# A transformer layer on one core: context's squares summed on VectorE, and three steps of attention and pooling asked for at other times

## The chip, the core and the metric

The kernel runs on one core of a Trainium2 chip. The metric is the device time in microseconds of one execution; lower is better. The core's engines work side by side: TensorE (PE in the profile, its weight loads PEld), VectorE (DVE), ScalarE (ACT), GpSimd (POOL), and SyncE (SP), which issues the transfers from HBM into the on-chip memory (SBUF). Matmuls write into PSUM, which has eight banks here.

## What is computed

One layer over 256 latent tokens and 256 context tokens, width 2048, all in float32. Cut to what matters:

```python
mod   = silu(c)     @ w_mod + b_mod          # sa, ca, ga, sm, cm, gm of the latent tokens
mod_c = silu(c_ctx) @ w_mod + b_mod
h_c = rmsnorm(ctx) * norm_attn_w * (1 + ca_c) + sa_c
h   = rmsnorm(x)   * norm_attn_w * (1 + ca)   + sa
# q, k, v, pooled input, gates: columns of h @ w_in; context gives keys and values only
q, k = rope(rmsnorm(q)), rope(rmsnorm(k));  k_c = rmsnorm(k_c)
heads = softmax(q1 k1^T) - lam * softmax(q2 k2^T), times v       # 8 heads, 512 keys
y_a = rmsnorm(heads) @ w_a_up
y_b = pool(p) @ w_b_up        # 4 groups: (mean over a window of 2, 4, 8, 16) - p, then a 256x256 product
x = x + ga * ((sigmoid(g_a) * y_a + sigmoid(g_b) * y_b) @ w_o)
x = x + gm * (relu(modulate(x) @ w_ff1) ** 2 @ w_ff2)
```

The norm `rmsnorm` divides by the root of the mean of squares over the 2048 channels of a token.

## The kernel before, in words

**Arithmetic.** A float32 weight chunk (128x1024, 512 KB) comes into a `raw` buffer (five of them), ScalarE casts it to a high part `whi` (line 224) and VectorE subtracts to get a low part `wlo` (line 225); a product is three matmuls of high and low parts. The raw buffer is free when the subtraction is done. For the modulation weights `w_m` the raw chunk itself is the matmul's operand.

**Order of the work.** The whole program is traced first, and then a planner of the framework gives every engine its own queue: of the instructions whose inputs its model of time takes as ready, the one earliest in the program goes first. So an instruction can get ahead of others that stand before it in the program. Three things hold that in check: instructions in `pin(...)` keep the program's order among themselves; with `ordered_pe` on, TensorE keeps the program's order altogether (it is on for the modulation stage and off after it); and a tile of a ring must wait until an earlier tile of that ring is given up. The ring `work` (tag `w2`) has nine buffers of 128x512 floats and serves nearly everything small: squares, raw keys, exponentials, pooled sums and differences. On the engine a queue is then worked off strictly in order.

**Transfers** are in one list (`plan`), which `load_next` walks; `wchunk` hands out the next chunk and loads two (at first three) chunks ahead. Each `wchunk` call is also one tick: `later(n, fn)` puts `fn` into the program n ticks on.

**Modulation stage** (loop over f = 0 to 15). `mod_tile(f)` takes four raw chunks and multiplies them with both conditioning vectors, and ScalarE copies the `rows` out (line 366). `mod_columns` turns rows into columns, and `hidden(f, t, ...)` makes slice f of the normed hidden tokens (lines 388 to 390), which needs `rms[t]`, the reciprocal root of the mean squares. `rms[0]` (latent) is made before the loop. Context arrives as four transfers `cT`, planned among the weights of f = 2 and 3. At f = 4 its squares are taken in four calls of `square_sums` (lines 459 to 469): two squares of 128x512 on ScalarE, their sum on VectorE, and two products with the constant matrix `mean` for each, so eight products of 128x256 add up in PSUM (`ssq`). Then come `rsq`, and context's slices 0 to 6 along with f = 4 to 6. Between the parts of an f, TensorE works off `steps`: products for keys and queries of group 0 (heads 0 to 3), as far as hidden slices are ready.

**Keys and queries.** `qk_evac` copies a product of 128 tokens out of PSUM, takes squares, norms and rotates, and `later(wait, turn)` asks for the four transposes (`qkT`, line 453) that bring it to `kT` or `qT`. After the modulation stage this is done for four key tiles (wait 2 + t) and two query tiles (6 + t). Meanwhile `v_group(0)` runs: eight chunks of `w_v`, 24 matmuls each (16 with the high part of the weights, eight with the low part).

**Main stretch.** `run(bulk, side, EVERY)` walks through the chunks of `q_group(1)`, `k_group(1)`, `v_group(1)`, `pooling()` and `gates()`. Every chunk yields a weight (0 for q, 4 for k and v, 2 in pooling and gates); whenever the sum has grown by EVERY = 4.4, one step of `attention` goes into the program: the scores of a head and 128 queries (`sc`, four matmuls), maxima on VectorE, exponentials on ScalarE, and the transposes (`aTp`) and value product (`ob`) of earlier steps. Steps of heads 4 to 7 must wait until all six tiles of group 1 are turned; such a step does nothing. At the same time `late_gen` streams the other modulation weights through VectorE (`macc`, line 581, pinned).

**Pooling.** For group g, four chunks of `w_p` give `pin` in PSUM. ScalarE copies it to `za`, GpSimd adds shifted copies (line 745) to window sums, and `later(3, ...)` asks for `pool_diff`: edge corrections on VectorE (line 757, pinned, at the start; line 759, not pinned, at the end), the difference `d` (line 761), and its split into `dh` (ScalarE, line 248) and `dl` (VectorE, line 249). `pool_out(g)` multiplies these with `pool_w`; groups 2 and 3 have it within the first chunks of `gates`.

After this come the output projection, the norm, and the MLP (`ff1`, `ff2`), which the diff does not touch.

Of the kernel before, what the change touches and what calls it, by code (L numbers as in the profile page):

```python
# [12 lines left out]
F32R = mybir.dt.float32r  # L13
# [7 lines left out]
T = 256  # L21
# [27 lines left out]
def layer(ctx: ExitStack, tc, a, out):  # L49
# [21 lines left out]
    def bank(name):  # L71
        return psum.tile([P, 512], F32, tag="ps", name=name)

    def work(name, shape=None, dt=F32):
        return pool.tile(shape or [P, 512], dt, tag="w2", name=name, bufs=9)
# [19 lines left out]
    def later(n, fn):  # L95

        waiting.append([n, fn])
# [284 lines left out]
    def hidden(f, t, c3):  # L382

        src, h = ((xT, hL), (cT, hC))[t]
        u = work("hw", [P, T])
        ht, k8 = h[f // 8], f % 8
        bias = c3[:, 1, t:t + 1]
        vec.scalar_tensor_tensor(u, src[:, f, :], c3[:, 0, t:t + 1], rms[t], ALU.mult, ALU.mult)
        act.activation(ht[:, 0, k8, :], u, AF.Identity, bias=bias)
        vec.scalar_tensor_tensor(ht[:, 1, k8, :], u, bias, ht[:, 0, k8, :].bitcast(F32), ALU.add, ALU.subtract)  # L390

    def tokens(nt):
        return [(hL, 0), (hL, 1), (hC, 0), (hC, 1)][:nt]
# [5 lines left out]
    def xstat(w, banks, toks, nk=8, last=1):  # L399

        for ch in range(nk - last + 1):
            n = last if ch == nk - last else 1
            chunks = [wchunk(*w, ch + i, ahead=AHEAD - i) for i in range(n)]
            order = [(i, kk, t) for i in range(n) for kk in range(2) for t in range(len(banks))]
            if ch == nk - last:
                order.sort(key=lambda o: o[2])
            groups = [order] if n == 1 else [[o for o in order if o[2] == t] for t in range(len(banks))]  # L410
            for group in groups:
                for part in range(2):
                    for i, kk, t in group:
                        k = 2 * (ch + i) + kk
                        h, tt = toks[t]
                        wt = chunks[i][part][:, kk * 512:kk * 512 + 512]
                        if part == 0:
                            pe.matmul(banks[t], tok(h, k, 0, tt), wt, start=k == 0, stop=False)  # L418
                            pe.matmul(banks[t], tok(h, k, 1, tt), wt, start=False, stop=False)  # L419
                        else:  # L420
                            pe.matmul(banks[t], tok(h, k, 0, tt), wt, start=False, stop=k == 2 * nk - 1)  # L421
            yield len(banks)
# [4 lines left out]
    def qk_evac(ps, tt, g, dest, tab, wait):  # L427
        raw = work("qraw")
        act.copy(raw, ps)
        sq = work("qsq")  # L430
        act.activation(sq, ps, AF.Square)
        ss = small("qss", 8)
        vec.reduce_sum(ss, sq.rearrange("p (h d) -> p h d", d=64), axis=AX.X)
        r = rsq(ss, 8, 1.0 / 64)
        r3 = raw.rearrange("p (h d) -> p h d", d=64)
        vec.tensor_mul(r3, r3, r.unsqueeze(2).broadcast_to([P, 8, 64]))
        if tt < 2:
            sq3 = sq.rearrange("p (h d) -> p h d", d=64)
            for ax in range(2):
                for b in range(2):  # L440
                    o = ax * 32 + b * 16
                    i = ax * 32 + (1 - b) * 16
                    vec.tensor_mul(sq3[:, :, o:o + 16], r3[:, :, i:i + 16],
                                   tabs[:, tab + 1, tt, o:o + 16].unsqueeze(1).broadcast_to([P, 8, 16]))
            vec.tensor_mul(r3, r3, tabs[:, tab, tt, :].unsqueeze(1).broadcast_to([P, 8, 64]))
            gp.tensor_add(raw, raw, sq)
        else:
            vec.tensor_mul(r3, r3, wkt.unsqueeze(1).broadcast_to([P, 8, 64]))

        def turn():  # L450
            pt = bank("qkT")
            for i in range(4):
                pin(pe.transpose(pt[:, i * P:i * P + P], raw[:, i * P:i * P + P], ident))
            act.copy(dest[:, 4 * g:4 * g + 4, tt * P:tt * P + P], pt.rearrange("p (i t) -> p i t", t=P))
            turned[g] += 1

        later(wait, turn)

    def square_sums(src, eng, sb, i):

        sq = [work("sq") for _ in range(2)]
        for h in range(2):
            k = 4 * i + 2 * h
            xs = src[:, k:k + 2, :].rearrange("p a t -> p (a t)")
            act.activation(sq[h], xs, AF.Square)
        eng.tensor_add(sq[0], sq[0], sq[1])
        return lambda: [pin(pe.matmul(sb[:, 0:T], mean, sq[0][:, h * T:h * T + T], start=(i + h == 0), stop=(i + h == 4)))
                        for h in range(2)]
# [25 lines left out]
    PACE = (0, 0, 4, 4, 6, 6, 8, 8) + (6,) * 8  # L494

    cols = {}

    context = {4: (0, 1), 5: (2, 3, 4), 6: (5, 6)}
    ordered_pe[0] = True
# [4 lines left out]
    for f in range(KT):  # L504
        if f % 2 == 0:
            ps = bank("mod")
        rows = mod_tile(f, ps)
        if f == 4:
            sb = bank("ssq")
            for i in range(4):  # L510
                square_sums(cT, vec, sb, i)()
            rms.append(rsq(sb[:, 0:T], T, P / D, "rms"))
        j = 2 if f == 6 else -1 if f == 5 or f % 2 == 0 else f // 2
        if j >= 0:
            for w in ("w_k", "w_q"):
                held[w, j] = wchunk(w, 0, j, ahead=FIRST_AHEAD if j < 7 else 1)
        steps(PACE[f] // 2)
        cols[f] = mod_columns(f, rows)
        steps(PACE[f] - PACE[f] // 2)
        hidden(f, 0, cols[f])  # L520
        for k in context.get(f, (f,) if f > 6 else ()):
            hidden(k, 1, cols[k])
        if f == 10:
            tables()
    lasts = [pair_steps(n, 7) for n in ("kx", "q", "kc")]
# [6 lines left out]
    qT = s8("qT", [P, NH, T])  # L532
    kT = s16("kT", [P, NH, 2 * T])
    for t in range(4):
        qk_evac(kb[t], t, 0, kT, 2, 2 + t)
    for t in range(2):
        qk_evac(qb[t], t, 0, qT, 0, 6 + t)

# [73 lines left out]

    def v_group(g):
        bs = [bank(f"v{g}_{t}") for t in range(4)]
        yield from xstat(("w_v", g), bs, tokens(4))
        for t in range(4):
            act.copy(v[:, t, g * 512:g * 512 + 512], bs[t])
        values[0] += 4
# [99 lines left out]
    def pooling():  # L718
        yb = pairtile("yb")
        ybh[0] = yb  # L720
        diff.clear()
        for g, w in enumerate(WINDOWS):
            ps = bank("pin")
            for i in range(2):
                for kc in range(2):
                    hi, lo = wchunk("w_p", 2 * g + i, kc)
                    for kk in range(8):
                        k = 8 * kc + kk
                        sl = slice(kk * P, kk * P + P)
                        mm3(ps[:, i * T:i * T + T], hi[:, sl], lo[:, sl], act_slice(hL, k, 0), act_slice(hL, k, 1),  # L730
                            k == 0, k == KT - 1)
                    if g > 1 and i == 0 and kc == 1:
                        pool_out(g - 2)
                    yield 2
            s0 = 8 - w // 2
            sums = []
            for i in range(2):
                src, oth = work("za", [P, T + 16]), work("zb", [P, T + 16])
                gp.memset(src[:, 0:8], 0.0)
                gp.memset(src[:, T + 8:T + 16], 0.0)  # L740
                act.copy(src[:, 8:T + 8], ps[:, i * T:i * T + T])
                step, n = 1, T + 16
                while step < w:
                    n -= step
                    gp.tensor_add(oth[:, 0:n], src[:, 0:n], src[:, step:step + n])
                    src, oth = oth, src
                    step *= 2
                sums.append(src[:, s0:s0 + T])
            later(3, partial(pool_diff, g, w, ps, sums))

    def pool_diff(g, w, ps, sums):

        d = work("d")
        n0, n1 = w // 2, w // 2 - 1
        e0 = PRM["edge"][0] + sum(x - 1 for x in WINDOWS[:g]) * 2
        for i, s in enumerate(sums):
            pin(vec.tensor_mul(s[:, 0:n0], s[:, 0:n0], prm[:, e0:e0 + n0]))
            if n1:
                vec.tensor_mul(s[:, T - n1:T], s[:, T - n1:T], prm[:, e0 + n0:e0 + n0 + n1])
            sl = slice(i * T, i * T + T)  # L760
            vec.scalar_tensor_tensor(d[:, sl], s, 1.0 / w, ps[:, sl], ALU.mult, ALU.subtract)
        dh = work("dh", dt=F32R)
        dl = work("dl", dt=F32R)
        split(dh, dl, d)
        diff.append((dh, dl))

    def pool_out(g):
        dh, dl = diff[g]
# [322 lines left out]
```

## Time and profile before

| | us |
|---|---|
| median of 3 runs | 1505.93 (1504.83 to 1506.88) |
| the profiled execution | 1506.33 |
| its span, first to last instruction | 1504.5 |
| TensorE busy | 1457.1 |
| VectorE busy | 992.0 |
| ScalarE busy | 694.6 |
| GpSimd busy | 120.7 |
| mean granted clock of TensorE | 0.991 |

Times in the views are microseconds from the span's start, and a timeline line reads: start, duration, engine, source line, operation, output <- inputs, shape, count; in brackets the idle time of the engine just before, and what ended it. Several like instructions in a row are one line with a count (x8); its duration then runs from the first start to the last end. L67 is the wrapper through which instructions with a written-out order go. Modulation lasts until about 143 us, the values of group 0 until 197, pooling and gates of group 0 until about 460, and from there on TensorE hardly waits.

### The profile page before, as it was taken

The page shows a single profiled execution, that of the slowest core. Times are in us where ns is not written, and L with a number is a line of the kernel's source. Part 1 is how long each engine was busy: PE and PEld are TensorE (multiplying, and loading weights), DVE is VectorE, ACT ScalarE, POOL GpSimd, SP SyncE. Part 2 cuts the span into 40 slices and gives each one's busy share as a digit, 9 for nine tenths or more (in the row PEclk, how much of TensorE's full clock was granted, in tenths as well). Part 3 has the DMA queues.
Part 4 walks back from the last instruction along what each step waited for, and adds up shares of the span by engine and source line. Part 5 has one row for each costly group of instructions (what it writes and reads, how often), then busy time and mean ns, then how long its engine had stood idle before and what let it go on. Part 6 is the DMA issues. An engine that isn't in the chain of part 4 may idle for free.

```text
span 1504.5 us, 20036 instructions
## 1 busy us (share of the span) xinstructions
PE 1457.1 (97%) x7592; PEld 1205.5 (80%) x7592; DVE 992.0 (66%) x1216; ACT 694.6 (46%) x956; POOL 120.7 (8%) x120
## 2 busy tenths in 40 slices
PE   5899999999899999999989999999999999999998
PEld 3567787678878888888879988888888888888887
DVE  3465968877877776666766765666666555555575
ACT  3334344646654444444534545535445453544532
POOL 0000101100320000000000100100000010000260
PEclk8999999999999999999999999999999999999999
DMA  9798687366578778788756677677776666656564
GB/s 377 296 345 324 195 284 247 98 210 208 169 234 295 255 262 273 249 304 282 213 159 203 226 247 239 210 248 229 246 236 215 192 189 194 188 192 193 186 194 141
DMA packets 97440, 347.85 MB, mean 231 GB/s; under 512 B 11072, under 2 KB 11712, under 8 KB 97344
## 3 DMA queue, kind: packets, MB, share of 16 engines
q1 hardware_dynamic: 96768, 345.50, 69.6%
q8 instruction: 59, 0.97, 0.3%
q0 software_dynamic: 576, 1.08, 0.2%
q14 instruction: 37, 0.30, 0.1%
HBM read 344.44 MB, written 2.10 MB: 230 GB/s over the span
## 4 chain that ended last, share of the span: by engine, by line
PE 87%; DVE 4%; DMA 4%; ACT 2%; issue 1%; POOL 1%; SPq 0%; DVEq 0%; ACTq 0%; POOLq 0%
PE f L940 14%; PE f L419 8%; PE f L418 8%; PE f L421 8%; PE f L943 7%; PE pg L419 3%; PE pg L418 3%; PE pg L421 3%; DMA raw<-in_w_m_dram 2%; PE w_k L67 2%; PE wo L419 2%; PE wo L421 2%; PE wo L418 2%; PE pyy L418 2%; PE pyy L419 2%; PE pyy L421 2%
## 5 line engine op out<-in xcount | busy, mean ns | idle before, releaser
L225 DVE TENSOR_TENSOR wlo<-raw,whi 128x1024 fp32r<-128x1024 f32 x443 | 547.9, 1239 | 360.4 <-ACT whi L224 337.6
L224 ACT CAST whi<-raw 128x1024 fp32r<-128x1024 f32 x443 | 463.9, 1048 | 574.2 <-PE f L419 184.9
L940 PE MATMUL f<-h,whi 128*128 128x512 f32 x896 | 224.2, 392 | 0.0
L418 PE MATMUL f<-whi,act 128*128 128x512 f32 x512 | 199.4, 389 | 0.0
L419 PE MATMUL f<-whi,act 128*128 128x512 f32 x512 | 199.3, 389 | 0.0
L940 PEld LDWEIGHTS f<-h,whi 128*128 128x128 f32 x896 | 161.7, 189 | 29.3
L581 DVE SCALAR_TENSOR_TENSOR macc<-raw,sil,macc 128x1024 f32<-128x1024 f32 x128 | 167.5, 1308 | 2.2 <-DMA macc<-in_b_ga_dram 1.9
L421 PE MATMUL f<-wlo,act 128*128 128x512 f32 x512 | 136.8, 389 | 0.0
L943 PEld LDWEIGHTS f<-h,wlo 128*128 128x128 f32 x896 | 122.3, 190 | 8.7
L943 PE MATMUL f<-h,wlo 128*128 128x256 f32 x896 | 124.9, 282 | 0.0
L421 PEld LDWEIGHTS f<-wlo,act 128*128 128x128 f32 x512 | 96.1, 188 | 19.9
L418 PEld LDWEIGHTS f<-whi,act 128*128 128x128 f32 x512 | 96.2, 188 | 19.9
L419 PEld LDWEIGHTS f<-whi,act 128*128 128x128 f32 x512 | 96.2, 188 | 19.7
L418 PE MATMUL pg<-whi,hL 128*128 128x512 f32 x256 | 100.6, 393 | 0.0
L419 PE MATMUL pg<-whi,hL 128*128 128x512 f32 x256 | 99.7, 390 | 0.0
L951 POOL TENSOR_TENSOR rsq<-relu 128x512 f32<-128x512 f32 x28 | 29.1, 1041 | 537.2 <-ACT relu L950 516.9
L421 PE MATMUL pg<-wlo,hL 128*128 128x512 f32 x256 | 68.6, 390 | 1.9 <-DVE wlo L225 1.9
L421 PEld LDWEIGHTS pg<-wlo,hL 128*128 128x128 f32 x256 | 48.0, 188 | 12.3 <-DVE wlo L225 2.4
L418 PEld LDWEIGHTS pg<-whi,hL 128*128 128x128 f32 x256 | 48.1, 188 | 10.1 <-issue 0.2
L419 PEld LDWEIGHTS pg<-whi,hL 128*128 128x128 f32 x256 | 48.1, 188 | 10.1 <-issue 0.2
L418 PE MATMUL wo<-whi,mix 128*128 128x512 f32 x128 | 49.9, 390 | 0.0
L419 PE MATMUL wo<-whi,mix 128*128 128x512 f32 x128 | 49.8, 389 | 0.0
(251 smaller groups left out, 2111.3 us busy)
## 6 DMA issues: line engine op xcount, KB each, us to landing
raw<-in_w_ff_dram SPq DMA_DIRECT2D x240, 512.0 KB, 4.3
raw<-in_w_m_dram SPq DMA_DIRECT2D x64, 512.0 KB, 8.0
raw<-in_w_ga_dram SPq DMA_DIRECT2D x32, 512.0 KB, 4.6
raw<-in_w_cm_dram SPq DMA_DIRECT2D x32, 512.0 KB, 4.4
raw<-in_w_gb_in_dram SPq DMA_DIRECT2D x32, 512.0 KB, 4.5
raw<-in_w_ga_in_dram SPq DMA_DIRECT2D x32, 512.0 KB, 4.7
raw<-in_w_sm_dram SPq DMA_DIRECT2D x32, 512.0 KB, 4.8
raw<-in_w_o_dram SPq DMA_DIRECT2D x32, 512.0 KB, 4.3
```

The costliest lines, as they stand in the source:

```text
L67: return (lambda *a, **k: pin(emit(*a, **k))) if self.flag[0] else emit
L224: act.copy(hi, raw)
L225: vec.tensor_sub(lo, raw, hi.bitcast(F32))
L418: pe.matmul(banks[t], tok(h, k, 0, tt), wt, start=k == 0, stop=False)
L419: pe.matmul(banks[t], tok(h, k, 1, tt), wt, start=False, stop=False)
L421: pe.matmul(banks[t], tok(h, k, 0, tt), wt, start=False, stop=k == 2 * nk - 1)
L581: pin(vec.scalar_tensor_tensor(acc, raw, sil[:, 0, k:k + 1], acc, ALU.mult, ALU.add))
L940: pe.matmul(ps, hi[:, kk * P:kk * P + P], both(h2, k), start=k == 0, stop=False)
L943: pe.matmul(ps[:, T:2 * T], lo[:, kk * P:kk * P + P], act_slice(h2, k, 0), start=False, stop=k == KT - 1)
L951: gp.tensor_mul(sq, r, r)
```

## The change

Four edits. Context's squares are taken by a new function `context_squares(i)`, called for quarters 0 and 1 after f = 2 and for quarters 2 and 3 after f = 3; VectorE keeps a running sum in one 128x512 tile, folds it to 128x256 at f = 4, and one product with `mean` follows. The key tiles of group 0 are turned a tick later. In `v_group(1)` the first two chunks yield the weights 0 and 2 instead of 4 and 4. The difference of pooling group 3 is asked for six ticks on instead of three, and the split of every group's difference is asked for one tick after the difference.

```diff
     cols = {}
+    total = []
+
+    def context_squares(i):
+
+        sq = [work("sq") for _ in range(2)]
+        for h in range(2):
+            act.activation(sq[h], cT[:, 4 * i + 2 * h:4 * i + 2 * h + 2, :].rearrange("p a t -> p (a t)"), AF.Square)
+        vec.tensor_add(sq[0], sq[0], sq[1])
+        if total:
+            vec.tensor_add(total[0], total[0], sq[0])
+        else:
+            total.append(sq[0])
...
         if f == 4:
+            sq = total[0]
+            vec.tensor_add(sq[:, 0:T], sq[:, 0:T], sq[:, T:2 * T])
             sb = bank("ssq")
-            for i in range(4):
-                square_sums(cT, vec, sb, i)()
+            pe.matmul(sb[:, 0:T], mean, sq[:, 0:T], start=True, stop=True)
             rms.append(rsq(sb[:, 0:T], T, P / D, "rms"))
...
             hidden(k, 1, cols[k])
+        if f in (2, 3):
+            for i in range(2):
+                context_squares(2 * f - 4 + i)
...
     for t in range(4):
-        qk_evac(kb[t], t, 0, kT, 2, 2 + t)
+        qk_evac(kb[t], t, 0, kT, 2, 3 + t)
...
         bs = [bank(f"v{g}_{t}") for t in range(4)]
-        yield from xstat(("w_v", g), bs, tokens(4))
+        for ch, w in enumerate(xstat(("w_v", g), bs, tokens(4))):
+
+            yield w if g == 0 or ch > 1 else 2 * ch
...
-            later(3, partial(pool_diff, g, w, ps, sums))
+            later(3 if g < 3 else 6, partial(pool_diff, g, w, ps, sums))
...
-        dh = work("dh", dt=F32R)
-        dl = work("dl", dt=F32R)
-        split(dh, dl, d)
-        diff.append((dh, dl))
+        diff.append((work("dh", dt=F32R), work("dl", dt=F32R)))
+        later(1, partial(split, *diff[-1], d))
```

## The prediction

> **What bounds the kernel now.** I read the page first, then the waits of TensorE, then the timeline at each place that the diff touches.
>
> ```profile
> span 1504.5 us, 20036 instructions
> PE 1457.1 (97%) x7592; PEld 1205.5 (80%) x7592; DVE 992.0 (66%) x1216; ACT 694.6 (46%) x956; POOL 120.7 (8%) x120
> PEclk8999999999999999999999999999999999999999
> PE 87%; DVE 4%; DMA 4%; ACT 2%; issue 1%; POOL 1%; SPq 0%; DVEq 0%; ACTq 0%; POOLq 0%
> ```
>
> TensorE is busy 1457.1 of 1504.5 us and makes 87% of the chain that ends last. Work taken off another engine gains nothing by itself; a change gains what it takes out of TensorE's queue or out of TensorE's waits. The waits of TensorE, in total us, times, and longest:
>
> ```profile
> PE mod L67 <- DMA raw<-in_w_m_dram: 13.5, 16, 3.0
> PE ssq L67 <- DVE sq L466: 9.6, 2, 7.2
> PE pin L254 <- DVE wlo L225: 4.3, 2, 2.9
> PE qkT L453 <- POOL qraw L446: 2.8, 3, 1.3
> PE sc L647 <- ACT e L652: 2.0, 1, 2.0
> PE pg L421 <- DVE wlo L225: 1.9, 1, 1.9
> PE sc L647 <- ACT qsq L431: 0.9, 1, 0.9
> ```
>
> Each part of the diff stands beside one of these rows: the squares beside ssq, the later turns of the keys beside qkT, the attention weights beside the two sc rows, the pooled differences beside pin and pg.
>
> **Part 1, context's squares.** This is the stretch of TensorE's queue in which the order is written out (the fourth slice of modulation weights, then the mean of squares, then the steps of keys and queries):
>
> ```profile
> 42.14 0.51 ACT L389 ACTIVATE hL<-hw,col 128x256 fp32r<-128x256 f32 x1 [1.14 <-DVE hw L388]
> 42.55 1.03 ACT L224 CAST first<-raw 128x1024 fp32r<-128x1024 f32 x1
> ...
> 43.61 1.23 DVE L225 TENSOR_TENSOR first<-raw,first 128x1024 fp32r<-128x1024 f32 x1 [0.45 <-ACT first L224]
> ...
> 44.87 4.67 SPq L212 DMA_DIRECT2D raw<-in_w_m_dram  x9
> ...
> 48.50 0.64 PE L67 MATMUL mod<-raw,cv 128*32 128x256 f32 x8 [2.01 <-DMA raw<-in_w_m_dram]
> 49.21 0.37 ACT L366 COPY rows<-mod 128x256 f32<-128x256 f32 x1 [4.68 <-PE mod L67]
> 49.47 3.75 ACT L465 ACTIVATE sq<-cT 128x512 f32<-128x512 f32 x7
> ...
> 51.49 6.35 PE L67 MATMUL ssq<-sq,mean 128*128 128x256 f32 x16 [2.35 <-DVE sq L466]
> ...
> 57.50 2.42 PE L67 MATMUL w_k<-first,hL 128*128 128x512 f32 x9
> ...
> 62.34 1.94 PE L67 MATMUL mod<-raw,cv 128*32 128x256 f32 x32
> ```
>
> TensorE ends f = 4 at 48.50 + 0.64 = 49.1, waits 2.35 us for squares that ScalarE begins only behind the copy of that f's rows, and then spends 6.35 us on 16 passes (two to each of eight products, 6.35 / 16 = 0.40 each). The diff leaves one product, two passes, 0.80 us, and puts the squares behind f = 2 and f = 3. Are they there in time? (An issue, the DMA view's line of context with its median us to landing, two lines of ScalarE's timeline, and the adds in the tile view with min/median/max ns.)
>
> ```profile
> 29.25 0.33 SPq L206 DMA_DIRECT2D cT<-in_cT_dram  x1
> ...
> cT<-in_cT_dram SPq DMA_DIRECT2D x4, 512.0 KB, 9.4
> ...
> 35.54 0.51 ACT L389 ACTIVATE hL<-hw,col 128x256 fp32r<-128x256 f32 x1 [1.14 <-DVE hw L388]
> ...
> 38.94 0.37 ACT L366 COPY rows<-mod 128x256 f32<-128x256 f32 x1 [2.90 <-PE mod L67]
> ...
> L466 DVE TENSOR_TENSOR sq<-sq x8: 691/692/693, 6.5 to 54.2; 128x512 f32<-128x512 f32 x8
> ```
>
> Context's last quarter is asked for at 29.25 and takes 9.4, so all of it lies there at 38.7. The first four squares fit on ScalarE between 36.05 (end of f = 2's last instruction) and 38.94: four by 3.75 / 7 = 0.54 is 2.14. The other four come behind 42.65; the last transfer that TensorE awaits lands at 48.50. VectorE's seven adds and one of half the width are 7 x 0.69 + about 0.4 = 5.2 us, against four adds, 2.8, now; it has 36 to 49 for them with little else. Their cover is that wait on DMA; were it gone, the last four squares and their adds would show, some 3 us.
>
> The cost is that the squares of f = 3 and the cast of the first key weights (42.55) want ScalarE in the same moment. That cast and its subtraction (43.61 to 44.84) free the raw buffer into which the transfer of 44.87 goes, and this is the one that lands at 48.50. Each square that gets ahead of it moves everything by 0.54; the cast stands earlier in the program, so I count one: TensorE begins ssq at 49.6 and ends at 50.4.
>
> Then the clock. Windows in rows: length, busy PE, PEld, DVE, ACT, POOL, granted clock, DMA share, GB/s.
>
> ```profile
> 46.70:50.10 3.40, 0.64 (x8) 0.16 (x8) 0.00 (x0) 0.89 (x3) 0.00 (x0) 0.99 0.99 377
> 50.10:53.50 3.40, 2.01 (x5) 1.67 (x6) 2.08 (x3) 3.12 (x7) 0.00 (x0) 0.50 1.03 417
> 53.50:57.00 3.50, 3.50 (x10) 2.75 (x9) 0.69 (x1) 0.63 (x1) 0.00 (x0) 0.52 1.02 406
> ...
> 64.00:70.00 6.00, 6.00 (x50) 4.43 (x46) 2.76 (x8) 2.32 (x6) 0.00 (x0) 1.00 0.49 175
> ...
> 398.30:401.70 3.40, 3.40 (x16) 3.40 (x17) 3.36 (x4) 3.40 (x10) 0.35 (x1) 0.51 0.74 230
> ```
>
> From 50.1 to 57.0 the clock is 0.5, and the ssq passes run in it. Without them the key steps stand in that low time. From 57.50 to 62.34 they and their company take 4.84 us at full clock. If the clock comes back at 53.5, then 50.4 to 53.5 does 1.55 of it, 3.29 is left, and f = 5 starts at 56.8 instead of 62.34: 5.5 us. If it comes back at 57.0, as before, 3.3 is done by then, f = 5 starts at 58.5: 3.8. If it never drops, 55.2: 7.1. I take 5.5, since after the stall near 398 one full window sufficed, and here the first window is now full too. The Trainium skill, "TensorE: Matmul & The Clock Gate", Part 1 on the clock gate, speaks against part of the gain: what is issued in the first 3.4 us or so after idling runs at half rate, and one busy window restores it. By that rule the sum has 5.5, by the rows at 50 to 57 it would have 3.8; the row of 398.30 agrees with the rule.
>
> Is it kept? The transfers for f = 5 to 7 were queued from 44.87 on, and 64 to 70 shows the DMA half idle (0.49), waiting for buffers that TensorE frees. From there on each wait for w_m follows TensorE's own releases, so all of it moves together. Counted: 5.5, bounds 3.0 (four squares ahead of the cast: ssq at 51.25 to 52.05, two low windows, f = 5 at 59.3) and 7.1.
>
> **Part 2, keys of group 0 turned a chunk later.**
>
> ```profile
> 157.15 0.66 PE L453 MATMUL qkT<-prm,qraw 128*128 128x128 f32 x4 [1.31 <-POOL qraw L446]
> 162.13 0.65 PE L453 MATMUL qkT<-prm,qraw 128*128 128x128 f32 x4 [0.89 <-POOL qraw L446]
> ```
>
> The two transposes stand 4.98 us apart, about one chunk of w_v; a chunk later covers 1.31 and 0.89. The last key now falls due with the first query, and attention starts only in k_group(1), so nobody waits for them. A qraw buffer is held 5 us longer. Gain 2.2; bounds a loss of 1.3 (one more wait of that size, for a buffer) and 2.2.
>
> **Part 3, attention pauses.** In v_group(1) the weights 4, 4 of the first two chunks become 0, 2; EVERY is 4.4. Summed, the seventh and eighth steps move from chunks 1 and 2 to chunks 3 and 4. The ninth and tenth steps were empty before (they waited for group 1's turns); now only the ninth is, so head 4 begins after chunk 6 as before, and every later step comes 0 or 1 chunk later. What it moves away from:
>
> ```profile
> 282.19 1.12 PE L647 MATMUL sc<-kT,qT 64*128 64x512 f32 x2 [0.88 <-ACT qsq L431]
> ...
> 286.86 1.12 PE L647 MATMUL sc<-kT,qT 64*128 64x512 f32 x2 [1.97 <-ACT e L652]
> 289.67 0.67 DVE L448 TENSOR_TENSOR qraw<-qraw,wkt 128x512 f32<-128x512 f32 x1
> ```
>
> The first scores wait for a PSUM bank that the last key's square still reads, the second for VectorE's maxima, which queue among the keys' norms; these end at 290.3. Three chunks in, both are past. Gain 0.88 + 1.97 = 2.85; bounds a loss of 2.0 (one more wait of that size, with the turns of chunks 3 to 6) and 2.85.
>
> **Part 4, pooling.** Group 3's difference is asked for six chunks on instead of three, each group's cast one chunk after its difference.
>
> ```profile
> 425.82 0.58 DVE L759 TENSOR_TENSOR za<-za,prm 128x7 f32<-128x7 f32 x1 [2.53 <-POOL za L745]
> 429.27 0.17 DVE L759 TENSOR_TENSOR za<-za,prm 128x7 f32<-128x7 f32 x1 [2.87 <-POOL za L745]
> 429.38 1.23 DVE L225 TENSOR_TENSOR wlo<-raw,whi 128x1024 fp32r<-128x1024 f32 x1
> 430.66 1.20 PE L421 MATMUL pg<-wlo,hL 128*128 128x512 f32 x4 [1.94 <-DVE wlo L225]
> ```
>
> VectorE stands 2.53 + 2.87 us at edge products whose sums GpSimd has not done; the gate weights' low part is queued behind them, and TensorE waits 1.94. L759 is not pinned and takes no new buffer, so the planner may put it there again: I take half, 1.0. The other side: sums, differences and casts hold their buffers of the nine-deep work ring longer, while heads come up to a chunk later. A new stall there would be priced like the longest in the pin row, 2.9, with a window at half clock behind it (398.30: 3.4 us, 1.7 lost): 4.6. Bounds: gain 2, loss 4.6.
>
> **The sum.** 5.5 + 2.2 + 2.85 + 1.0 = 11.55. The profiled execution took 1506.33 (span 1504.5 and 1.83 around it), 0.40 above the median of the runs, 1505.93. So 1494.8 for the like of that execution, 1494.4 for the median.
>
> **Rivals.**
> *The squares do not move.* ScalarE took no square before the rows of f = 4, though all of context was there at 38.7; if what held them (the work ring hands out buffers in program order) is not it, they run at 49.47 again, seven adds behind them, and the one product ends near 57.4 instead of 57.84. Part 1 gives 0.4, the time 1499.5. Against it: they now stand ahead of f = 4's rows in the program.
> *The casts go behind the squares.* The bound of 3.0 in part 1: 1496.9. It decides as soon as the planner thinks the key weights land after hL of f = 3.
> *Slower.* Part 4's longer-held buffers: every group's copy out of PSUM and every difference needs work buffers that the previous group's cast gives back. With a cast a chunk later at each of four groups, a weight's low part is stuck behind a difference each time: 4 x 4.6 = 18.4, less 10.55 of the other parts, 1513.8. It decides from three such stalls on (13.8 against 10.55 + 3). For it: pin and pg show that this already happens three times. Against: they are three in the whole kernel, 6.2 us, and heads come at most one chunk later.
>
> **How the numbers follow.** Forecast 0.60, squares unmoved 0.12, casts behind squares 0.13, slower 0.08, and 0.07 for pooling losses that about cancel the gain. The range: below, part 1 at 7.1, pooling at 2 and some more shifting, 1490; above, part 1 at 0.4, part 3 at nothing, 1502. A difference of 0.2%, 3 us, is about what a measurement here tells from none. Faster by more: 0.83; within: 0.09; slower: 0.08.
>
> **What would show it.** ssq for context as two passes right behind f = 4, without a wait on sq; w_k behind it partly at 0.5; f = 5 near 57. No qkT wait near 157 and 162. The scores of the seventh step near 285 on the new clock without waits. In pooling, L759 of width 7 without idle time ahead of it, pg waits gone. I am wrong if ssq still begins behind the rows' copy by 5 us or more, if the transfer that f = 4 awaits lands 2 us later than 48.5, or if new waits of TensorE between 380 and 460 add up to more than the 1.9 of pg.

## The result, and the profile after

The changed kernel takes 1490.85 us (median of 4 runs, 1490.53 to 1492.22) against 1506.41 of the kernel before beside it (1504.83 to 1509.66): a ratio of 0.9896, interval 0.9878 to 0.9913. That is 15.6 us where 11.5 were forecast; the time lies in the range, near its lower end. The profiled execution took 1492.22, 14.1 less than the one before. One execution below, the profiled one of the changed kernel with a transfer on GpSimd's queue, took 4145.31 us where its other five took 1491.66 to 1494.04; its ratio leaves it out, and its trace isn't used. The page of the changed kernel:

```profile
span 1490.4 us, 19996 instructions
...
PE 1450.0 (97%) x7578; PEld 1201.2 (81%) x7578; DVE 992.8 (67%) x1220; ACT 694.3 (47%) x956; POOL 121.2 (8%) x120
...
PE 90%; DMA 4%; DVE 3%; ACT 1%; issue 1%; SPq 1%; POOL 0%; DVEq 0%; POOLq 0%; ACTq 0%
```

VectorE and ScalarE do what they did, as squares and sums only moved. TensorE lost 14 passes of ssq and some slow ones. Its waits (us in total, times, longest):

```profile
PE mod L67 <- DMA raw<-in_w_m_dram: 15.6, 20, 2.3
PE ssq L67 <- DVE sq L466: 7.0, 1, 7.0
PE pin L254 <- DVE wlo L225: 5.6, 2, 3.3
...
PE late L617 <- ACT e L671: 1.5, 1, 1.5
```

The second wait for squares is gone (the one left is that of the latent tokens at the start), and so are qkT, both sc rows and pg (the gates' products). But w_m rose from 13.5 to 15.6 and pin from 4.3 to 5.6, and a wait of `late` (products that sum up the late modulation weights) of 1.5 stands where there was one of 0.5. Where the time went shows better by stretches between landmarks of TensorE's timeline, whose ends lie on the same instruction in both traces (us, each rounded by itself; forecast beside them):

| stretch | before | after | less | forecast |
|---|---|---|---|---|
| start to the end of f = 4 | 49.1 | 47.9 | 1.3 | 0 |
| end of f = 4 to first values | 98.8 | 95.5 | 3.4 | 5.5 |
| values to first queries of group 1 | 49.1 | 46.4 | 2.7 | 2.2 |
| queries to keys of group 1 | 22.7 | 22.7 | 0.0 | 0 |
| keys to first pin | 120.3 | 115.7 | 4.6 | 2.85 |
| first pin to the first product of `oT` | 138.5 | 136.9 | 1.6 | 1.0 |
| from there to the last product | 1020.9 | 1020.2 | 0.7 | 0 |

The first row is not the change's: among the traces of the kernels below, f = 4 ends anywhere from 47.9 to 50.2, with or without the squares' edit.

**The squares.** TensorE's timeline from f = 4 to f = 7 in the changed kernel (start, duration, instruction, count, and in brackets the idle time ahead of it and its releaser):

```profile
47.24 0.64 PE L67 MATMUL mod<-raw,cv 128*32 128x256 f32 x8 [2.00 <-DMA raw<-in_w_m_dram]
47.84 0.67 PE L67 MATMUL ssq<-sq,mean 128*128 128x256 f32 x2
48.16 3.98 PE L67 MATMUL w_k<-first,hL 128*128 128x512 f32 x9
...
54.60 1.93 PE L67 MATMUL mod<-raw,cv 128*32 128x256 f32 x32
...
69.21 1.07 PE L67 MATMUL mod<-raw,cv 128*32 128x256 f32 x16
71.14 0.64 PE L67 MATMUL mod<-raw,cv 128*32 128x256 f32 x8 [0.86 <-DMA raw<-in_w_m_dram]
72.42 0.64 PE L67 MATMUL mod<-raw,cv 128*32 128x256 f32 x8 [0.64 <-DMA raw<-in_w_m_dram]
```

The two passes stand right behind f = 4, with no wait; nine passes of w_k take 3.98 us instead of 2.42, since part of them runs at half clock (the granted clock is 0.50 from 48.6 to 52.0). From the end of f = 4 to f = 5 are 6.7 us, against 13.2 before: 6.5 gained. Only 3.4 are left when the values begin. f = 7, which ran through without waiting before, now waits twice for weights. SyncE's timeline says where these were (issues, start and time over which a group of them is issued), first before, then after:

```profile
49.80 0.33 SPq L115 DMA_DIRECT2D raw<-in_w_k_dram  x1
51.44 13.26 SPq L212 DMA_DIRECT2D raw<-in_w_m_dram  x4
69.66 0.33 SPq L115 DMA_DIRECT2D raw<-in_w_q_dram  x1
```

```profile
48.54 0.33 SPq L115 DMA_DIRECT2D raw<-in_w_k_dram  x1
61.93 0.33 SPq L115 DMA_DIRECT2D raw<-in_w_q_dram  x1
62.31 2.07 SPq L212 DMA_DIRECT2D raw<-in_w_m_dram  x4
```

The planner put a chunk of w_q (index 2, so the third; the expectations below call it the second) ahead of the four transfers of f = 7. It needs a raw buffer that f = 6 gives back, so SyncE stands from 48.9 to 61.9, and what is behind it stands too, though f = 7 has buffers of its own, free when f = 5 is done (54.60 + 1.93). This is the only difference in SyncE's order, and the prediction did not look for one.

### The profile page after: what moved, and what is told of

It reads as the page before. It is cut to its first block, busy times and chain, and to the rows that moved or that the text cites. A ratio compares the mean times of both kernels' runs of the same rounds, so it can differ in the third digit from the quotient of the medians.

```text
span 1490.4 us, 19996 instructions
## 1 busy us (share of the span) xinstructions
PE 1450.0 (97%) x7578; PEld 1201.2 (81%) x7578; DVE 992.8 (67%) x1220; ACT 694.3 (47%) x956; POOL 121.2 (8%) x120
## 4 chain that ended last, share of the span: by engine, by line
PE 90%; DMA 4%; DVE 3%; ACT 1%; issue 1%; SPq 1%; POOL 0%; DVEq 0%; POOLq 0%; ACTq 0%
PE f L957 14%; PE f L418 8%; PE f L419 8%; PE f L421 8%; PE f L960 7%; PE pg L419 4%; PE pg L418 4%; PE pg L421 4%; DMA raw<-in_w_m_dram 2%; PE wo L419 2%; PE wo L418 2%; PE wo L421 2%; PE pyy L418 2%; PE pyy L419 2%; PE pyy L421 2%; PE w_k L67 2%
## 5 line engine op out<-in xcount | busy, mean ns | idle before, releaser
L67 PE MATMUL mod<-raw,cv 128*32 128x256 f32 x512 | 36.5, 401 | 15.6 <-DMA raw<-in_w_m_dram 15.6
L418 PE MATMUL wo<-whi,mix 128*128 128x512 f32 x128 | 49.9, 390 | 0.0
```

The lines of the kernel that those rows point to most:

```text
L67: return (lambda *a, **k: pin(emit(*a, **k))) if self.flag[0] else emit
```

## Experiments: the four parts alone

Each part by itself on the kernel before. What a kernel gains in us is worked out from its ratio; by the medians it differs from that by up to 0.7.

**Squares alone.** (Only `context_squares`, its calls, the fold and the one product.)

```diff
-            for i in range(4):
-                square_sums(cT, vec, sb, i)()
+            pe.matmul(sb[:, 0:T], mean, sq[:, 0:T], start=True, stop=True)
...
+        if f in (2, 3):
+            for i in range(2):
+                context_squares(2 * f - 4 + i)
```

> Part 1 alone. Theory: the parts add, each taking away its own stall. In the changed kernel 6.5 us were gained between f = 4 and f = 5 (13.2 us from one to the other before, 6.7 after), and 3.1 were given back to waits on modulation weights at f = 7 and f = 10, because the second query chunk (buffer not free until f = 6) now stands ahead of the four transfers of f = 7 in SyncE's queue. So: f = 5 about 6.5 us sooner after f = 4, f = 7 split by DMA waits again, values begin 3.4 us sooner (4.6 with the 1.3 that the changed kernel's profile already led by at f = 4), the time 3.4 below before, 0.9977. Rival: the give-back comes from the other parts' rearranged queues; then part 1 alone keeps 6.5, 0.9957.

Measured: 1501.53, ratio 0.9978 (0.9967 to 0.9989), 3.3 us less. f = 7 waits again (0.62 and 0.63), with the same order in SyncE's queue; from the end of f = 4 to the values it is 95.2, where it was 98.8. So what part 1 brings is about 3.5, not what it had won at f = 5.

**Turns alone.**

```diff
-        qk_evac(kb[t], t, 0, kT, 2, 2 + t)
+        qk_evac(kb[t], t, 0, kT, 2, 3 + t)
```

> Part 2 alone. Theory: the waits of 1.31 and 0.89 for the two keys go and nothing comes in their place; the first product of group 1's queries comes 2.2 to 2.7 us sooner after the first product of values (49.0 us before, 46.4 in the changed kernel), the time 2.2 to 2.7 below before, 0.9983. Rival: raw keys held longer keep a query's copy waiting, and the transposes of queries wait instead; then under 1 us, 0.9995 or more.

Measured: 1503.36, ratio 0.9987 (0.9977 to 0.9997), 2.0 us less. This term stands.

**Pause alone.**

```diff
-        yield from xstat(("w_v", g), bs, tokens(4))
+        for ch, w in enumerate(xstat(("w_v", g), bs, tokens(4))):
+
+            yield w if g == 0 or ch > 1 else 2 * ch
```

> Part 3 alone. Theory: the two waits of score products (0.88 and 1.97) go; pooling begins about 4.5 us sooner after the keys of group 1 begin (120.3 us before, 115.8 in the changed kernel), of which some 2 us are attention's products moved behind that point; at the first product of the attention's output with w_a the lead is 2.85, and the time 2.85 below before, 0.9981. Rival: the later attention runs into pooling's queue and gives the 2.85 back as waits of pooling products for low parts; then 0.999 to 1.000.

Measured: 1498.72, ratio 0.9951 (0.9936 to 0.9966), 7.4 us less (5.1 to 9.6), over two and a half times the forecast of 2.85. TensorE's waits in this kernel:

```profile
PE pd L252 <- ACT whi L224: 2.9, 1, 2.9
PE late L600 <- ACT e L654: 1.6, 1, 1.6
...
PE pin L254 <- DVE wlo L225: 0.4, 1, 0.4
```

Both sc waits are gone, as said; but also pg is gone and pin is down from 4.3 to 0.4, at the price of one wait of pd (the product with `pool_w`). Nothing in pooling was edited here. So the size of the theory fell, and two questions follow, taken up in the next section.

**Pooling alone.**

```diff
-            later(3, partial(pool_diff, g, w, ps, sums))
+            later(3 if g < 3 else 6, partial(pool_diff, g, w, ps, sums))
...
-        split(dh, dl, d)
...
+        later(1, partial(split, *diff[-1], d))
```

> Part 4 alone. Theory as predicted: the wait of 1.94 for the gate weights' low part goes in whole or half, 1 to 2 us below before, 0.9990; VectorE still stands at the two edge products of width 7, since they need no new buffer. Rival: the changed kernel's lead in this stretch comes from attention's new places alone, and part 4 alone gives 0 or up to 2 us more.

Measured: 1504.63, ratio 0.9991 (0.9978 to 1.0004): no difference to be told. The wait of pg is still there with 1.9, and from the values to the last product it is 1351.3 against 1351.4.

**All but pooling**: the changed kernel with part 4 taken back.

```diff
-            later(3 if g < 3 else 6, partial(pool_diff, g, w, ps, sums))
+            later(3, partial(pool_diff, g, w, ps, sums))
...
-        later(1, partial(split, *diff[-1], d))
...
+        split(dh, dl, d)
```

> Parts 1, 2 and 3 without part 4. Part 4 alone measured 0.9991 with an interval over 1, and its profile still has the wait of 1.94 for the gate weights. Theory: part 4 gives nothing and in the changed kernel only moves waits (pin waits 5.6 us there, 0.4 and one of 2.9 with part 3 alone), so without it the time is that of the changed kernel within 2 us, 0.9885 to 0.9905 of before. Rival: together with part 3 it does take a stall away, and without it the time is 2 us or more above the changed kernel, 0.991 or more.

Measured: 1490.33, ratio 0.9899 (0.9883 to 0.9915), the same as the whole change. Part 4 adds nothing to the others either. VectorE's timeline in the changed kernel shows why it couldn't:

```profile
409.96 0.57 DVE L778 TENSOR_TENSOR za<-za,prm 128x7 f32<-128x7 f32 x1 [3.12 <-POOL za L764]
411.35 0.17 DVE L778 TENSOR_TENSOR za<-za,prm 128x7 f32<-128x7 f32 x1 [0.82 <-POOL za L764]
...
412.10 1.22 DVE L225 TENSOR_TENSOR wlo<-raw,whi 128x1024 fp32r<-128x1024 f32 x1
```

L778 is L759 of before. Asked for three ticks later, the edge products of width 7 still stand ahead of sums that GpSimd has not done, VectorE still idles 3.12 + 0.82 there, and a weight's low part is queued behind them.

## Experiments: what the pause is worth

Two things change with the pause: where TensorE waits within the values of group 1, and which chunk of pooling each later step of attention falls on. The next two kernels do one without the other.

**The pause without the shift**: the steps wait as in the change, but the weights then catch up, so that in pooling they fall on the chunks of the kernel before.

```diff
+        for ch, w in enumerate(xstat(("w_v", g), bs, tokens(4))):
+            yield (0, 0, 7.5, 4.08)[ch] if g == 1 and ch < 4 else w
```

> Before with the pause alone: in v_group(1) the first chunks weigh 0, 0, 7.5 and 4.08, so the seventh and eighth steps come in chunks 3 and 4, and from then on every step stands at the same chunk as before. Part 3 alone measured 7.4 us. Theory: it has two halves, the waits of 2.85 and the half-clock windows that they bring in some executions (0 to 3.4 us, about 1.7), here kept: 4.5 us, 0.9970, with the pooling waits as before (pin 4.3, pg 1.9). Rival: all of the 7 us hang on the two waits; then 0.995.

Measured: 1501.09, ratio 0.9971 (0.9959 to 0.9982), 4.4 us less. Up to the first pin TensorE's queue has the order of the pause alone, and from there on that of the kernel before; the waits of pin and pg are those of before.

**The shift without the pause**: nothing is changed in the values, but pooling's first chunk weighs less, and from there on the steps fall where they do in the change.

```diff
-                    yield 2
+                    yield 0.4 if (g, i, kc) == (0, 0, 0) else 2
```

> Before with the shift alone: the first pooling chunk weighs 0.4 instead of 2, so that from there on every attention step stands at the chunk that it has in the changed kernel, and v_group(1) stays as before. Theory: the other half of part 3's gain, 2.7 us between the first pooling product and the first product with yb (104.9 us before, 102.2 with part 3 alone), 0.9982, with the score waits of 2.0 and 0.9 still there. Rival: pooling gains only when the keys' norms and the scores no longer collide ahead of it; then 0.9995 or more.

Measured: 1502.06, ratio 0.9973 (0.9962 to 0.9984), 4.1 us less. Here TensorE's queue has the order of the kernel before up to the first pin, and that of the pause alone from there on. The sc waits are still there, pg is gone, pin 1.0, pd 2.3. From first pin to the first product of oT it is 134.2 instead of 138.5, and TensorE's waits in it (those over 0.25) add up to 3.3 instead of 7.5: they carry the difference. So the 7.4 are two things of about the same size, 4.4 and 4.1, each known to about 1.7, and the larger surprise is that one weight of 2 turned into 0.4 is worth about as much as the whole pause.

For pg the rows show most of why. This is GpSimd's timeline around the last window sum (`za`), in the kernel before and then in this one:

```profile
427.06 1.49 POOL L682 TENSOR_SCALAR osq<-osq 128x512 f32<-128x512 f32 x1
428.51 0.73 POOL L745 TENSOR_TENSOR za<-zb 128x257 f32<-128x257 f32 x1
```

```profile
424.96 0.74 POOL L745 TENSOR_TENSOR za<-zb 128x257 f32<-128x257 f32 x1
...
433.49 1.90 POOL L682 TENSOR_SCALAR osq<-osq 128x512 f32<-128x512 f32 x1 [7.23 <-ACT osq L681]
```

`osq`, the squares of an output of attention, is attention's work on GpSimd. In the kernel before it stands ahead of the last sum. VectorE waits 2.87 us at the second edge product for that sum (429.27 in the prediction), and the low part that pg awaits is queued behind. With the steps shifted `osq` comes after the sum, and VectorE waits 0.23 there. The 1.49 us of `osq` are most of the 1.94 that pg waits. In all six traces with `osq` ahead of that sum pg waits 1.9 us; in the seven with `osq` behind it pg doesn't wait. What the shift does to pin and pd is not followed instruction by instruction.

The other surprise is that the pause alone brings 4.4 where its waits are 2.85. This kernel, with the waits still in it, shows part of it. TensorE's timeline behind the second wait (the same place in the kernel before is in the prediction, at 286.86), and windows over it (length, busy PE, PEld, DVE, ACT, POOL, granted clock, DMA share, GB/s):

```profile
287.18 2.05 PE L647 MATMUL sc<-kT,qT 64*128 64x512 f32 x2 [1.96 <-ACT e L652]
289.15 0.79 PE L418 MATMUL v<-whi,hC 128*128 128x512 f32 x1
289.75 0.63 PE L419 MATMUL v<-whi,hC 128*128 128x512 f32 x1
```

```profile
284.00:287.40 3.40, 1.45 (x7) 0.88 (x6) 3.40 (x6) 0.78 (x3) 1.58 (x1) 0.98 0.00 0
287.40:290.80 3.40, 3.40 (x7) 1.60 (x8) 3.40 (x9) 0.78 (x2) 0.00 (x0) 0.50 0.22 66
290.80:294.20 3.40, 3.40 (x11) 2.72 (x10) 1.28 (x2) 1.87 (x4) 0.00 (x0) 0.52 0.22 88
```

The same stretch of the kernel before, in the profile that the prediction read:

```profile
284.00:287.40 3.40, 1.43 (x6) 0.68 (x5) 3.40 (x8) 0.81 (x3) 1.37 (x1) 1.00 0.00 0
287.40:290.80 3.40, 3.40 (x17) 2.39 (x16) 3.40 (x7) 2.35 (x6) 0.00 (x0) 1.00 0.33 84
```

The same waits, 1.43 and 1.45 us of work in the first window; here the clock falls to half for two windows, there it doesn't fall. Two windows at half clock lose 3.4 at most. Of six traces with the waits in them (the kernel before, the three single parts that keep them, the shift, and one more below) two have 6.8 us at half clock behind them, two 3.4, and two none; of seven traces with the pause none has any. From the keys of group 1 to first pin it is 120.3 and 120.7 in the two without half clock, 121.3 and 122.4 with one window of it, 123.0 and 123.5 with two, and 115.7 to 117.1 in the seven. By these, two windows cost some 2.3 to 3.2, an estimate, since a qkT wait of up to 1.2 differs among them too. The profile of before was one of the two lucky ones.

Without any half clock the stretch still gains 4.6 in the change. 0.88 + 1.97 are the waits, and 0.6 a qkT wait that is gone. Against it stands the `late` wait, 1.54 where 0.53 was. Another part is in the scores themselves. In the kernel before, a wait stood between each two of four, and each two took 1.12; in the changed kernel:

```profile
285.11 1.13 PE L666 MATMUL sc<-kT,qT 64*128 64x512 f32 x4
```

All four take 1.13 when they stand together (their starts lie in pairs 0.01 us apart, so two scores run side by side, one on each half of the 128 rows), so splitting them cost another 1.1. That makes 0.88 + 1.97 + 0.6 - 1.0 + 1.1 = 3.5. The last 1.0 is in other products, which are as many as before but take up more time from start to start, waits left out: the 192 passes of v 46.1 us before and 45.2 after, the 24 of ob 5.0 and 4.8. What slows them is not shown.

## Experiments: where part 1's lead goes

**SyncE's order as before**: in the changed kernel, that chunk of w_q planned and asked for behind f = 7's weights.

```diff
+        if f == 7:
+            plan("w_q", 0, 2)
...
-            plan("w_q", 0, j)
+            if j != 2:
+                plan("w_q", 0, j)
...
+        if f == 7:
+            held["w_q", 2] = wchunk("w_q", 0, 2, ahead=FIRST_AHEAD)
...
```

> The changed kernel with the second query chunk planned behind the four weight transfers of f = 7, the order that SyncE's queue had before the change. Theory: the 3.1 us that part 1 gave back at f = 7 and f = 10 were this queue, so f = 7 has no DMA wait, values begin 2 to 3 us sooner than in the changed kernel, 0.9875 of before. Rival: the transfers are late because the DMA has too little time for them in any order; then f = 7 or f = 8 waits as long as now and the time is that of the changed kernel, 0.9896.

Measured: 1493.27, ratio 0.992 (0.9904 to 0.9936), 2.4 above the change's 1490.85, with intervals that overlap. SyncE's order is that of the kernel before, and f = 7's wait is gone, but its products now need that chunk sooner than it can be there:

```profile
70.12 1.93 PE L67 MATMUL mod<-raw,cv 128*32 128x256 f32 x32
...
73.49 0.49 PE L67 MATMUL w_q<-whi,hL 128*128 128x512 f32 x1 [1.44 <-ACT whi L227]
74.75 0.50 PE L67 MATMUL w_q<-wlo,hL 128*128 128x512 f32 x1 [0.77 <-DVE wlo L228]
```

From the start of f = 5 to the values it is 89.3, against 88.7 in the change. Late either way: the order alone is no cure. So the next kernel takes the chunk out of the queue altogether.

**That one transfer from GpSimd's queue**, idle between 3 and 150 us; no other instruction of any engine changes its place. Once on the whole change, once without part 4.

```diff
-    def raw_chunk(src, n=1024):
+    def raw_chunk(src, n=1024, queue=sp):
...
-        sp.dma_start(raw, src)
+        queue.dma_start(raw, src)
...
-        raw = raw_chunk(src, n)
+        raw = raw_chunk(src, n, gp if key == ("w_q", 0, 2) else sp)
```

> The whole change, with one DMA moved: the second chunk of w_q, which in the changed kernel stands in SyncE's queue ahead of the four w_m transfers of f = 7 and waits there for the raw buffer of f = 6 (asked for at 61.93, then w_m at 62.31 to 64.38), is issued from GpSimd's queue, empty between 3 and 150 us. Theory (the order of SyncE's queue costs the waits of f = 7): w_m of f = 7 is issued right behind f = 5, by about 57 to 59; f = 7 starts its 32 passes without waiting (0.86 + 0.64 now), no wait for w_q comes in its place, since that chunk is asked for at about 62 as now, and the first values begin 1.5 to 2.7 earlier than in the changed kernel, counted from the start of f = 5 (88.7 there): 86.0 to 87.2; time 1.5 to 2.7 below the change's 1490.85, a ratio of about 0.988 to 0.987 to the kernel before. Rival (the DMA itself is late, whatever the order): the waits stay at f = 7 or come at w_q, f = 5 to the values 88.7 again, ratio 0.9896 as the change.

> Parts 1 to 3 without the pooling part, and with the one w_q transfer on GpSimd's queue: the version that the experiments point to. Theory: as parts 1 to 3 alone (0.9899) less the 1.5 to 2.7 of the f = 7 wait: ratio 0.9881 to 0.9889. Rival (the waits only move): 0.9899.

Measured: 1493.43, ratio 0.9919 (0.9906 to 0.9933), on the whole change, and 1491.14, ratio 0.9905 (0.9892 to 0.9919), without part 4. These are rows of the second, SyncE's timeline and then TensorE's:

```profile
50.91 7.16 SPq L212 DMA_DIRECT2D raw<-in_w_m_dram  x4
```

```profile
55.71 1.93 PE L67 MATMUL mod<-raw,cv 128*32 128x256 f32 x32
...
70.31 1.93 PE L67 MATMUL mod<-raw,cv 128*32 128x256 f32 x32
...
78.30 1.50 PE L67 MATMUL mod<-raw,cv 128*32 128x256 f32 x24
80.30 0.64 PE L67 MATMUL mod<-raw,cv 128*32 128x256 f32 x8 [0.51 <-DMA raw<-in_w_m_dram]
...
93.75 0.64 PE L67 MATMUL mod<-raw,cv 128*32 128x256 f32 x8 [0.43 <-DMA raw<-in_w_m_dram]
95.03 0.64 PE L67 MATMUL mod<-raw,cv 128*32 128x256 f32 x8 [0.64 <-DMA raw<-in_w_m_dram]
```

The local claim holds: the weights of f = 7 are issued by 58 instead of 64, f = 7 runs through, and no wait for w_q comes in its place. But f = 8 waits 0.51 and f = 10 still 1.07. From the start of f = 5 to the values it is 87.3, against 88.2 in parts 1 to 3 and 88.7 in the change: 0.9 to 1.4 of the expected 1.5 to 2.7. In the time of the whole kernel nothing of it can be told (0.9905 against 0.9899), so this version does not beat the change.

**Fewer bytes.** What stops the lead next? From 72 us on the DMA was nearly full in the kernel before already (windows: length, busy PE, PEld, DVE, ACT, POOL, clock, DMA share, GB/s), and so it is after, once SyncE has stood still (0.41 from 56 to 64):

```profile
72.00:80.00 8.00, 8.00 (x62) 5.83 (x61) 5.64 (x12) 4.68 (x8) 0.00 (x0) 1.00 0.93 345
...
96.00:110.00 14.00, 13.70 (x110) 9.48 (x110) 7.62 (x20) 5.24 (x13) 0.00 (x0) 1.00 0.92 352
```

```profile
56.00:64.00 8.00, 8.00 (x70) 5.52 (x63) 3.74 (x10) 3.04 (x8) 0.00 (x0) 1.00 0.41 148
64.00:72.00 8.00, 6.92 (x50) 4.68 (x48) 5.22 (x10) 2.97 (x6) 0.00 (x0) 1.00 0.98 360
72.00:80.00 8.00, 7.58 (x52) 5.58 (x56) 4.52 (x8) 3.54 (x6) 0.00 (x0) 1.00 0.99 378
```

So five transfers are left out, in the changed kernel and in the one before:

```diff
-            plan("w_m", f, i)
+            if i < 3 or f < 7 or f % 2 == 0:
+                plan("w_m", f, i)
...
+        raws += raws[2:] if len(raws) < 4 else []
```

> The whole change, with five transfers of modulation weights left out: for f = 7, 9, 11, 13 and 15 the fourth slice is not loaded, and TensorE reads the third twice (so part of the modulation is not the reference's; TensorE's passes are as many as before). 2.5 MB less for the DMA between 60 and 130 us. Theory (from f = 5 on TensorE cannot keep its lead because the DMA moves 0.9 to 1.0 of what it can, in the kernel before too: 0.93 to 0.96 from 72 to 130): the waits for w_m behind f = 7 (0.61, 0.64, 0.34, 0.64) go; f = 7 may still wait for what stands behind w_q; from the start of f = 5 to the first values 84.4 to 85.9 (88.7 in the change). Rival (the lead is lost to something else, casts or buffers that follow TensorE): it stays near 88, 3 above the same edit of the kernel before. Time: 3 below the change, 1487.8, by the theory; 1490 by the rival.

> The kernel before, with the same five transfers left out. Theory: its three waits behind f = 5 (0.30, 0.65, 0.30) go, from the start of f = 5 to the first values 84.4 (85.7 in the kernel before), so that the change's lead at f = 5 (6.5 of it by the squares) is found whole at the first values once the bytes are fewer. Rival: 84.4 too, while the change's stays 3 longer. Time 1.3 below the kernel before: 1504.6.

Measured: the change with fewer bytes 1490.31, ratio 0.9896 (0.9877 to 0.9914); the kernel before with fewer bytes 1504.2, ratio 0.9991 (0.9979 to 1.0002). In the latter all waits behind f = 5 go, and to the values it is 83.6 instead of 85.6. In the former it is 86.8 instead of 88.7: 1.9 come back, but it stays 3.2 above the other, and that is the rival's number. Fewer bytes help both kernels alike; they don't give the lead back. But the DMA isn't free for it either: in the change with fewer bytes its share is still 0.97 from 96 to 110 us and 0.99 from 110 to 124, so this pair of kernels does not tell a full DMA from the ring of buffers below. The remaining waits of that kernel are 0.71 at f = 7 (behind w_q, as in the change), 0.26 at f = 10, and 1.55 at f = 14. The last is a row of TensorE's timeline:

```profile
123.36 0.64 PE L67 MATMUL mod<-raw,cv 128*32 128x256 f32 x8 [1.55 <-DMA raw<-in_w_m_dram]
```

What leads up to it, in the timeline of ScalarE and VectorE, and then in SyncE's:

```profile
114.39 1.05 ACT L225 CAST first<-raw 128x1024 fp32r<-128x1024 f32 x1 [0.60 <-DMA raw<-in_w_k_dram]
115.46 1.22 DVE L226 TENSOR_TENSOR first<-raw,first 128x1024 fp32r<-128x1024 f32 x1 [1.16 <-ACT first L225]
```

```profile
116.72 0.33 SPq L213 DMA_DIRECT2D raw<-in_w_m_dram  x1
```

Even f take their weights in the ring of five raw buffers, and the fourth slice of an even f takes the buffer that a key chunk had. The last slice of f = 14 is issued at 116.72, as soon as the subtraction of that chunk (115.46 + 1.22) has ended, and it lands 6.6 later, at 123.31. The subtraction stood behind the cast, and the cast behind the landing of the key chunk. What TensorE meets there is this round of landing, cast, subtraction and next transfer. It hardly comes sooner when TensorE is early: the same slice lands at 123.63 in the kernel before with fewer bytes, where f = 5 began 4.3 us later. For the one slice this is read off the rows. All waits for w_m over 0.2 us behind f = 7, in the changed kernel and in the one before, stand at f = 10, 12 and 14, all but one of them at that fourth slice; that the ring takes the rest of the lead is still argued, not shown. A sixth buffer wasn't tried.

## Why the prediction came out as it did

**What bounds the kernel: right.** All that was gained came out of TensorE's queue (14 passes of ssq), its waits and its slow passes; VectorE's and ScalarE's busy time is the same.

**Part 1, the squares at f = 5: right, a little small.** The squares ran behind f = 2 and f = 3 and beside the first cast, ssq was two passes without a wait, w_k took the low clock, and f = 5 came 6.5 sooner, 5.5 forecast. Of the two cases weighed there, the rule of the Trainium skill ("TensorE: Matmul & The Clock Gate", Part 1: one busy window brings the clock back) came nearer than the 3.8 by the rows at 50 to 57: in the changed kernel's trace the clock is at half for 3.4 us behind f = 4. In four other traces with the squares' edit it is 6.8, begun before f = 4 ended, and there too f = 5 starts 6.4 to 7.2 behind the end of f = 4. Nothing is seen of the 0.54 counted for a square ahead of the cast.

**Part 1, "Is it kept?": wrong.** It said that from f = 5 on each wait for w_m follows TensorE's own releases, so all of it moves together. It read one window, 64 to 70, in which the DMA is half idle, and not those behind it, where it is at 0.92 to 0.96. 3.4 of 6.5 stayed (3.3 by the time of the squares alone). Two places are shown: f = 7, whose weights stand behind a transfer that waits for its buffer in SyncE's queue (0.9 to 1.4 net), and, with fewer bytes, the last slice of f = 14, which can't be asked for before a key chunk gives its raw buffer back. Whether the ring or a DMA that is nearly full takes the rest stays open. The prediction took SyncE's order as given, where the planner makes it anew.

**Part 2: right.** 2.7 in the stretch and 2.0 alone, for 2.2; no turn of keys waits for GpSimd between 154 and 172.

**Part 3: right in kind, the size wrong.** The scores of the seventh step stand at 285.11, without waits, as said. The term of 2.85 measured 7.4 alone: 4.4 in its own place, as the waits also split the scores and, in four of six traces, brought half clock behind them; and 4.1 in pooling, by steps that come up to a chunk later, which for one thing take attention's `osq` out of the way of pooling's sums on GpSimd. The prediction had noted that shift and priced it at nothing, except as a risk.

**Part 4: wrong, and small.** The 1.0 were half of pg's 1.94, since the planner might put L759 where it was; it did, idle time and all. More than half of the 2.87 was `osq` ahead of the last sum on GpSimd, which the prediction did not look for. The pg wait went by part 3's shift: it is gone in the pause alone and in the shift alone, and still there in pooling alone and in the pause without the shift. By the traces part 4 may even cost something once the steps are shifted: first pin to oT is 134.2 to 135.1 in the four kernels with the shift and without part 4, and 135.4 to 136.9 in the three with both; TensorE's waits in it add up to 3.3 to 3.7 and to 4.0 to 5.8. In the time this can't be told: of the two pairs that differ in part 4 alone, 1491.14 and 1493.43 point the same way with intervals that overlap, and the ratios 0.9899 and 0.9896 show nothing.

**The slower rival** needed three stalls of 4.6 in pooling. The pin waits grew by 1.3 in all, and pg's 1.9 went; it failed on the number of its stalls and on their size.

So the sum was near for a poor reason: part 1 fell short by about 2 and part 4 by 1.0, part 3 came out about 4.5 over, and the profiled execution had a start 1.3 us sooner. That is luck, not a sum that held. The four parts alone add up to 3.3 + 2.0 + 7.4 + 1.4 = 14.1, the whole to 15.7 (0.0104 of 1506.41; interval 13.1 to 18.4): they add, within what can be measured.

## What to carry to other kernels

A lead won early in a stage of loads is kept only as far as the loads can follow: look at the DMA's share window by window up to the end of the stage, and at the order in the issuing queue, where one transfer that waits for its buffer holds up all behind it. A short stall of TensorE costs its length, what it splits, and sometimes a window or two of half clock, which a single profile may or may not show. When work that is paced by weights is put off, price it where it lands too; here that was worth as much as the wait it was put off for. And look at the order on the engines that seem idle too: GpSimd is busy 8% of the time, yet one instruction of 1.49 us ahead of a sum there made most of a wait of 1.9 in TensorE.

## What the runs showed of the hardware

Waits of 0.88 and 1.97 us in five, with work between them, were followed by no low clock in two traces, 3.4 us of it in two, and 6.8 us in two, with the same instructions around them: by the stretch around them a price of 0 to some 3 us for one stall. Two passes of scores of 64x512 on 64 rows took 1.12 us alone, and four passes in a row, which started in pairs, 1.13. While one transfer waited for its buffer, SyncE issued nothing for 13 us (48.9 to 61.9), and the DMA's share fell to 0.41 (56 to 64).
